# Query and key norms read their sum of squares from an SBUF copy, sample values are transposed three slots later, and the chunk pool has ten buffers

## The chip, the cores and the metric

The kernel runs on one core of one Trainium2 chip. The metric is the time of one execution in device microseconds (us); lower is better. Three runs of the kernel before gave 2138.12, 2135.49 and 2138.64 us, so the median is 2138.12 us.

## What is computed

One step of a decoder layer, for a prompt of 1024 tokens and for 8 samples of 4 tokens each. All 1056 tokens share the weights. The part that matters here is the norm of queries and keys and what attention does with them:

```python
xn = rms_norm(x, norm1_g) * (1 + scale1) + shift1
h, b_gate, c_gate, q, k, v, g_conv, g_att = jnp.split(jnp.dot(xn, w_in), split_at, axis=-1)
...
shp = (nb, ns, N_GROUPS, HEADS_PER_GROUP, HEAD_DIM)      # 3 groups, 8 heads, 64
q = rms_norm(q.reshape(shp), q_norm_g)
k = rms_norm(k.reshape(shp), k_norm_g)
...
if decode: o, lse, kb, vb = dilated_attn_decode(...)     # samples: cache plus new keys and values
else:      o, lse = dilated_attn_prompt(...)             # prompt: blocks of 128, window 128
...
x = x + gate1 * jnp.dot(sigmoid(g_conv) * conv_out + sigmoid(g_att) * attn_out, w_o)
x = x + gate2 * jnp.dot(relu(jnp.dot(xn2, w_mlp_in)) ** 2, w_mlp_out)
```

## The kernel before

Tokens lie along the free dimension in three column chunks of 352, features along the 128 partitions. Each fp32 product is split into a high and a low part, so one output tile of 128 features by 352 tokens takes 24 matmuls of 352 columns (`gemm`, L377: high by high, low by high, high by low, for eight blocks of 128). The stages run one behind the other: modulation and first gates, the convolution inputs, **queries, keys and values with attention beside them** (from about 515 to 1148 us of the profile), the convolution's output product (to about 1283 us), attention's output product, `w_o`, and the two halves of the MLP.

The stage in question goes over 12 units (three attention groups, four pairs of heads each), and in a unit over a query, a key and a value tile with three chunks each. Work beside the matmuls is put into *slots*: `slot()` is called in the middle and at the end of every `gemm`. It runs the functions in `self.later` whose count has run down, then a piece of the attention generator (`bg`), then the paced generators (`decode` for the samples, `merge` for the prompt). Each engine runs what it is given in that order.

A query or key chunk (`qk_epilogue`) has four steps. Right behind its matmuls ScalarE (ACT) writes the squares (`sq`, L688) and copies the raw values (L689) out of the PSUM bank `ps_g`. One slot later VectorE (DVE) splits the squares into a high and a low part (`halves`: `sqh` L160, `sql` L162). Three slots later (`stats`) TensorE (PE) sums the squares over each head with two matmuls (L380, L381) into the PSUM bank `ps_ss`, of which there is **one**, and ACT computes Ln (L389, reads `ps_ss`), Exp (L390) and Square (L391). Another slot later (`scale`) DVE refines the reciprocal root: L395 reads `ps_ss` again, L396 and L706 follow. The bank is free for the next chunk's L380 when L395 has read it.

When a unit's values are done, `begin` calls `sample_values` (a transposition of 32 columns through the PSUM bank `ps_pt`, copied to `vnew` by ACT or DVE as `evac` picks) and then queues the unit's attention. In a group's fourth unit `sample_values` also queues `decode(g)`. `ps_pt`, also a single bank, serves the transpositions of attention (`values`, `att_tr`) too. `chunk()` hands out tiles of 352 columns from a pool with 8 buffers; the epilogues, the decode steps and the gate loads `sg` of the output product live in it. All loads and stores beside a few at the start are issued by SyncE (SP) in program order.

Of the kernel before, what the change touches and what calls it, by code (L numbers as in the profile page):

```python
# [11 lines left out]
AF = mybir.ActivationFunctionType  # L12
ALU = mybir.AluOpType
# [18 lines left out]
EPS = 1e-6  # L32
# [17 lines left out]
class Trunk:  # L50
    def __init__(self, ctx, tc, t):
        self.tc, self.nc, self.t = tc, tc.nc, t
        pool = lambda **kw: ctx.enter_context(tc.tile_pool(**kw))
        self.cp = pool(name="const", bufs=1)
        self.pg = pool(name="pages", bufs=NPG)
        self.ck = pool(name="chunks", bufs=8)
        self.wp = pool(name="weights", bufs=3)
        self.sm = pool(name="small", bufs=3)
        self.pp = pool(name="psum", bufs=1, space=PSUM)
        self.dp = pool(name="scratch", bufs=1, space=DRAM)  # L60
        self.bg = deque()
        self.paced = [deque(), deque()]
        self.pause = [0, 0]
        self.credit = 0.0
        self.rate = 0.0
        self.items = deque()
        self.ready = set()
        self.bias = None
        self.done = False
        self.work = 0.0  # L70
        self.later = []
        self.act_load = 0.0
        self.dve_load = 0.0
# [607 lines left out]
    def qk_epilogue(self, is_k, g, j, c, ps, st):  # L681
        nc = self.nc
        if c == 0:
            st["n"] = self.page("kn" if is_k else "qn")
        qn = st["n"]
        qc = qn[:, c * CH:(c + 1) * CH]
        sq = self.chunk("sq")
        nc.scalar.activation(sq, ps[:, :CH], AF.Square)  # L688
        nc.scalar.copy(qc, ps[:, :CH])  # L689
        h = []  # L690

        def halves():
            h.extend(self.chunk(n, dt=F32R) for n in ("sqh", "sql"))
            self.split(h[0], h[1], sq, CH, hi_on="dve")

        def stats():
            ss = self.bank("ss")[:, :CH]
            self.sumsq_mm(ss, self.blk_r, h[0], h[1], True, True)
            h.clear()
            r0 = self.chunk("r0")  # L700
            self.rstd_a(ss, sq, r0, self.eps[:, 1:2])
            self.later.append((1, lambda: scale(ss, r0)))

        def scale(ss, r0):
            self.rstd_b(r0, ss, sq, r0, 64 * EPS)
            nc.vector.scalar_tensor_tensor(  # L706
                out=qc, in0=qc, scalar=self.qkg[:, is_k:is_k + 1], in1=r0, op0=ALU.mult, op1=ALU.mult)
            if c == 2:
                self.later.append((1, finish))

        def finish():
            hi, lo = self.page("hi", (P, NP), F32R), self.page("lo", (P, NP), F32R)
            st["hi"], st["lo"] = hi, lo
            if g == 0:
                self.split(hi, lo, qn[:, 0:NP], NP, lo_on="pool")
            else:
                d = DIL[g]
                h3, l3 = (a.rearrange("p (r a) -> p r a", r=d) for a in (hi, lo))
                self.split(h3, l3, qn[:, 0:NP].rearrange("p (a r) -> p r a", r=d), NP, lo_on="pool")
            nc.vector.tensor_copy(self.samp[is_k][:, 4 * g + j, :], qn[:, NP:T])  # L720
            if is_k:
                w = (P, 512, NP)[g]
                self.later.append((3, lambda: nc.sync.dma_start(out=self.t["k_out"][g][j], in_=qn[:, NP - w:T])))

        self.later.append((1, halves))
        self.later.append((3, stats))

    def store_v(self, g, j, page):
# [558 lines left out]
    def run(self):  # L1287
        nc, t, c = self.nc, self.t, self.cp
# [47 lines left out]
        st = {}  # L1336
# [18 lines left out]
        st = {}  # L1355
        yc = {}

        def begin(g, j, st):
            self.sample_values(g, j, st["v"]["v"])
            self.add_unit(g, j, st["q"], st["k"], st["v"]["v"])  # L1360
            if (g, j) == units[-1]:
                self.done = True
                self.rate = 2000.0
            else:
                self.rate = self.work / 18 * 0.85

        for ji in range(ji, nb):
            kd, g, j = jobs[ji]
            for ch in range(NCH):
                s = slice(ch * CH, (ch + 1) * CH)  # L1370
                ps = self.bank("g")
                self.gemm(ps[:, :CH], self.wt[ji], range(KD), [(self.xh[k][:, s], self.xl[k][:, s]) for k in range(KD)])
                if ch == 0:
                    st[kd] = {}
                if kd in "qk":
                    self.qk_epilogue(int(kd == "k"), g, j, ch, ps, st[kd])
                else:
                    self.v_epilogue(g, j, ch, ps, st["v"])
                del ps
                if ch == 0:  # L1380
                    self.prep_to(ji + 1, True)
                    if kd == "k":
                        self.bias = self.load_bias(g, j)
                if kd == "v" and ch == 2:
                    self.later.append((2, lambda g=g, j=j, st=st: begin(g, j, st)))
                    st = {}
                if ch == 2:
                    self.wt.pop(ji)
                if (kd, g, j) == ("k", ORDER[2], 3) and ch == 2:
                    yc[0] = self.conv_ops(0)  # L1390
                self.slot()
# [249 lines left out]
        def scale(m, a, t):  # L1641
            k = 2 * H - 32 * t
            nc.scalar.activation(a[:, :k], a[:, :k], AF.Copy, scale=gate2[:, m, 0:1])
            if t:
                s = a[:, k:].rearrange("p (b t) -> p b t", t=NT)
                nc.vector.tensor_tensor(out=s, in0=s, in1=gate2[:, m, 1:9].unsqueeze(2).to_broadcast([P, NB, NT]), op=ALU.mult)
# [60 lines left out]
        g = 0  # L1707
# [35 lines left out]
        for n, (m, ch) in enumerate([(m, ch) for m in (4, 5, 6, 7, 0, 1, 2, 3) for ch in range(NCH)]):  # L1743
            j, s = m % 2, slice(ch * CH, (ch + 1) * CH)
# [230 lines left out]
```

## Time and profile before

| | |
|---|---|
| median of three runs | 2138.12 us |
| profiled execution | 2140.99 us, span 2139.2 us |
| PE busy | 2026.4 us (95%) |
| DVE, ACT, POOL busy | 1422.8, 998.2, 777.5 us (67%, 47%, 36%) |
| mean granted TensorE clock | 0.983 of full speed |

The profile is of one execution; its own time is 2.87 us above the median of the three runs. A busy share is a mean over stages. What a wait costs is read in its stage: from the list of who waited for whom on PE, and from the timeline around the wait. In a timeline row the square brackets at the end give the idle time of the engine just before the instruction, and what ended it.

### The profile page before, as it was taken

What the parts mean: (1) busy time and instruction counts of PE and PEld (TensorE: products, weight loads), DVE (VectorE), ACT (ScalarE), POOL (GpSimd) and SP (SyncE); (2) the same over time, 40 slices, a digit from 0 to 9 for tenths busy, and PEclk for the clock granted to TensorE, in tenths of its full rate; (3) what the DMA queues carried; (4) which work ended last, traced back from release to release, by engine and by line L of the source; (5) the groups of instructions that cost most, each with busy time, mean ns of one, the idle gap of its engine ahead of it and who ended that gap; (6) DMA issues with size and microseconds to landing.
All of it is one profiled execution on the core that took longest, in us unless ns stands there. A gap on an engine that the chain in (4) does not pass through costs nothing. (4 is left out here: it accounts for less than half of the span.)

```text
span 2139.2 us, 38867 instructions
## 1 busy us (share of the span) xinstructions
PE 2026.4 (95%) x15092; PEld 1903.0 (89%) x15092; DVE 1422.8 (67%) x2944; ACT 998.2 (47%) x2193; POOL 777.5 (36%) x544
## 2 busy tenths in 40 slices
PE   5899999999999999999999989999999999999998
PEld 2799999889989888888888889989999998999998
DVE  4847766444666655566676677678444447999997
ACT  4623332434656655555555233455555557433332
POOL 3645655331111111100011114234323335887785
PEclk8899999999999999999999999999999999999999
DMA  7242312664112343433247875642356639555542
GB/s 287 65 144 81 101 62 79 239 218 155 56 56 64 121 127 130 129 124 127 83 144 247 274 254 176 211 148 98 122 200 242 252 115 347 205 207 200 180 166 97
DMA packets 143376, 338.69 MB, mean 158 GB/s; under 512 B 34392, under 2 KB 81112, under 8 KB 142168
## 3 DMA queue, kind: packets, MB, share of 16 engines
q1 hardware_dynamic: 142760, 336.01, 46.5%
q8 instruction: 118, 1.93, 0.4%
q14 instruction: 66, 0.54, 0.1%
q10 hardware_dynamic: 432, 0.20, 0.0%
HBM read 279.00 MB, written 116.39 MB: 185 GB/s over the span
## 5 line engine op out<-in xcount | busy, mean ns | idle before, releaser
L162 DVE TENSOR_TENSOR wprod<-wraw,wprod 128x512 fp32r<-128x512 f32 x276 | 275.0, 997 | 171.5 <-ACT wprod L158 169.9
L377 PE MATMUL ps_g<-xh,whi 128*128 128x352 f32 x1056 | 357.4, 338 | 8.0 <-DVE graw L99 3.8
L377 PE MATMUL ps_g<-xh,wlo 128*128 128x352 f32 x1056 | 346.5, 328 | 7.1 <-DVE wlo L200 7.1
L377 PE MATMUL ps_g<-xl,whi 128*128 128x352 f32 x1056 | 346.3, 328 | 2.4 <-POOL xl L406 1.7
L377 PEld LDWEIGHTS ps_g<-xh,whi 128*128 128x128 f32 x1056 | 203.0, 192 | 32.9 <-issue 13.2
L158 ACT CAST wprod<-wraw 128x512 fp32r<-128x512 f32 x276 | 163.3, 618 | 134.4 <-DVE wprod L162 104.5
L377 PEld LDWEIGHTS ps_g<-xh,wlo 128*128 128x128 f32 x1056 | 202.6, 192 | 8.5 <-DVE wlo L200 8.5
L377 PEld LDWEIGHTS ps_g<-xl,whi 128*128 128x128 f32 x1056 | 203.7, 193 | 4.9 <-POOL xl L406 3.4
L200 DVE TENSOR_TENSOR wlo<-wraw,whi 128x512 fp32r<-128x512 f32 x200 | 152.5, 803 | 50.0 <-ACT whi L193 49.6
L162 POOL TENSOR_TENSOR lo<-qn,hi 128x1024 fp32r<-128x1024 f32 x12 | 32.9, 2739 | 361.7 <-ACT hi L158 326.1
L277 POOL TENSOR_TENSOR ps_z<-ps_z,ps_s 128x264 f32<-128x264 f32 x64 | 63.9, 1001 | 254.4 <-DVE ps_s L276 254.3
L264 PE MATMUL ps_s<-th,wprod 128*128 128x264 f32 x512 | 146.5, 286 | 1.7 <-DVE ps_s L276 1.7
L264 PE MATMUL ps_g<-th,wprod 128*128 128x264 f32 x512 | 146.9, 287 | 0.0
L266 PE MATMUL ps_g<-th,wprod 128*128 128x264 f32 x512 | 146.0, 285 | 0.0
L265 PE MATMUL ps_s<-tl,wprod 128*128 128x264 f32 x512 | 145.9, 285 | 0.0
L265 PE MATMUL ps_g<-tl,wprod 128*128 128x264 f32 x512 | 145.8, 285 | 0.0
L266 PE MATMUL ps_s<-th,wprod 128*128 128x264 f32 x512 | 145.5, 284 | 0.0
L994 ACT ACTIVATE S<-S,ng 128x128 f32<-128x128 f32 (+1 forms) x192 | 84.2, 440 | 111.2 <-DVE ng L989 111.2
L193 ACT CAST whi<-wraw 128x512 fp32r<-128x512 f32 x200 | 113.3, 618 | 41.3 <-DMA wraw<-in_w_conv_out 27.3
L264 PE MATMUL ps_g<-xh,wprod 128*128 128x264 f32 x384 | 110.0, 287 | 2.9 <-ACT wprod L158 2.9
L264 PE MATMUL ps_s<-xh,wprod 128*128 128x264 f32 x384 | 109.3, 285 | 3.4 <-DVE ps_s L280 3.4
L266 PE MATMUL ps_g<-xh,wprod 128*128 128x264 f32 x384 | 109.8, 286 | 0.2 <-DVE wprod L162 0.2
(382 smaller groups left out, 6424.9 us busy)
## 6 DMA issues: line engine op xcount, KB each, us to landing
wraw<-in_w_in SPq DMA_DIRECT2D x76, 512.0 KB, 4.3
wada<-in_w_ada SPq DMA_DIRECT2D x48, 512.0 KB, 5.4
hid_d<-hid SPq DMA_DIRECT2D x32, 528.0 KB, 4.0
wraw<-in_w_mlp_in SPq DMA_DIRECT2D x32, 512.0 KB, 5.6
wraw<-in_w_mlp_out SPq DMA_DIRECT2D x32, 512.0 KB, 3.8
hraw<-hid_d SPq DMA_DIRECT2D x56, 264.0 KB, 4.5
kv<-in_v SPq DMA_DIRECT2D x28, 512.0 KB, 5.9
wraw<-in_w_conv_out SPq DMA_DIRECT2D x24, 512.0 KB, 7.0
```

Source lines behind the costliest of these rows:

```text
L158: nc.scalar.copy(hi, src)
L162: eng.tensor_tensor(out=lo, in0=src, in1=hi.bitcast(F32), op=ALU.subtract)
L193: self.nc.scalar.copy(hi[:, s], w[:, s])
L200: self.nc.vector.tensor_tensor(out=lo[:, s], in0=w[:, s], in1=hi[:, s].bitcast(F32), op=ALU.subtract)
L264: nc.tensor.matmul(ps, hi, xh, start=(k == 0), stop=False)
L265: nc.tensor.matmul(ps, hi, xl, start=False, stop=False)
L266: nc.tensor.matmul(ps, lo, xh, start=False, stop=(k == 3))
L277: nc.gpsimd.tensor_tensor(out=z[p], in0=z[p], in1=s[p], op=ALU.add)
L377: self.nc.tensor.matmul(ps, a, x, start=(i == 0), stop=(i == n - 1))
L994: nc.scalar.activation(s, s, AF.Exp, bias=ng[:, hh, i:i + 1], accum_out=sm[:, hh, i:i + 1])
```

## The change

Three edits. `ScalarE` copies `ps_ss` plus the small constant into `sq` first (L701, Identity), and the rest of the norm, on ACT and on DVE, reads that copy; the intermediate values get a chunk tile `tmp` of their own. `sample_values` is put off by three slots. The chunk pool has ten buffers. No reciprocal root, no matmul and no transfer is added or dropped.

```diff
-        self.ck = pool(name="chunks", bufs=8)
+        self.ck = pool(name="chunks", bufs=10)
...
             h.clear()
-            r0 = self.chunk("r0")
-            self.rstd_a(ss, sq, r0, self.eps[:, 1:2])
-            self.later.append((1, lambda: scale(ss, r0)))
-
-        def scale(ss, r0):
-            self.rstd_b(r0, ss, sq, r0, 64 * EPS)
+            r0, tmp = self.chunk("r0"), self.chunk("tmp")
+            nc.scalar.activation(sq, ss, AF.Identity, bias=self.eps[:, 1:2])
+            nc.scalar.activation(tmp, sq, AF.Ln)
+            nc.scalar.activation(r0, tmp, AF.Exp, scale=-0.5)
+            nc.scalar.activation(tmp, r0, AF.Square, scale=float(0.5 ** 0.5))
+            self.later.append((1, lambda: scale(r0, tmp)))
+
+        def scale(r0, tmp):
+            nc.vector.tensor_tensor(out=tmp, in0=sq, in1=tmp, op=ALU.mult)
+            nc.vector.scalar_tensor_tensor(out=r0, in0=tmp, scalar=1.5, in1=r0, op0=ALU.subtract, op1=ALU.mult)
             nc.vector.scalar_tensor_tensor(
                 out=qc, in0=qc, scalar=self.qkg[:, is_k:is_k + 1], in1=r0, op0=ALU.mult, op1=ALU.mult)
...
         def begin(g, j, st):
-            self.sample_values(g, j, st["v"]["v"])
+            self.later.append((3, lambda: self.sample_values(g, j, st["v"]["v"])))
             self.add_unit(g, j, st["q"], st["k"], st["v"]["v"])
```

How the instructions stand on the engines is shown at three places. The first is ACT at the first two query chunks behind the fourth unit, whose sample values are among those that ACT evacuates (`whi` is a weight's high part, `r` the tile `r0`). Before:

```order
L96 COPY vnew<-ps_pt 32x128
L688 ACTIVATE sq<-ps_g 128x352
L689 COPY qn<-ps_g 128x352
L193 CAST whi<-wraw 128x512 x2
L688 ACTIVATE sq<-ps_g 128x352
L689 COPY qn<-ps_g 128x352
L389 ACTIVATE sq<-ps_ss,eps 128x352
L390 ACTIVATE r_8394<-sq 128x352
L391 ACTIVATE sq<-r_8394 128x352
```

and now:

```order
L688 ACTIVATE sq<-ps_g 128x352
L689 COPY qn<-ps_g 128x352
L193 CAST whi<-wraw 128x512 x2
L688 ACTIVATE sq<-ps_g 128x352
L689 COPY qn<-ps_g 128x352
L96 COPY vnew<-ps_pt 32x128
L701 ACTIVATE sq<-ps_ss,eps 128x352
L702 ACTIVATE tmp<-sq 128x352
L703 ACTIVATE r_8444<-tmp 128x352
L704 ACTIVATE tmp<-r_8444 128x352
```

The copy of the sample values has moved behind the squares and raw copies of two chunks, and four ACT instructions stand where three stood.

The second place is PE in the fifth unit, where the statistics of a query chunk are followed by the transposed values of the unit before (`values`, four transpositions in `ps_pt` and four in `ps_g`). Before:

```order
L377 MATMUL ps_g<-xh,wlo 128x352
L380 MATMUL ps_ss<-sqh,blk_r 128x352
L381 MATMUL ps_ss<-sql,blk_r 128x352
L102 MATMUL ps_pt<-ident,v 128x128 x4
L102 MATMUL ps_g<-ident,v 128x128 x4
L377 MATMUL ps_g<-xh,whi 128x352
```

and now:

```order
L377 MATMUL ps_g<-xh,wlo 128x352
L102 MATMUL ps_pt<-ident,v 32x128
L380 MATMUL ps_ss<-sqh,blk_r 128x352
L381 MATMUL ps_ss<-sql,blk_r 128x352
L102 MATMUL ps_pt<-ident,v 128x128 x4
L102 MATMUL ps_g<-ident,v 128x128 x4
L377 MATMUL ps_g<-xh,whi 128x352
```

The sample transposition, which stood 38 rows further up, now stands two matmuls ahead of the next use of `ps_pt`.

The third place is DVE in the first query tile, from the halves of one chunk to the scaling of the chunk ahead of it. Before:

```order
L160 CAST sqh<-sq 128x352
L162 TENSOR_TENSOR sql<-sq,sqh 128x352
L395 SCALAR_TENSOR_TENSOR sq<-ps_ss,sq 128x352
L396 SCALAR_TENSOR_TENSOR r_5688<-sq,r_5688 128x352
L706 SCALAR_TENSOR_TENSOR qn<-qn,qkg,r_5688 128x352
```

and now:

```order
L160 CAST sqh<-sq 128x352
L162 TENSOR_TENSOR sql<-sq,sqh 128x352
L708 TENSOR_TENSOR tmp<-sq,tmp 128x352
L709 SCALAR_TENSOR_TENSOR r_5688<-tmp,r_5688 128x352
L710 SCALAR_TENSOR_TENSOR qn<-qn,qkg,r_5688 128x352
```

The count and the places of the DVE instructions are the same; the first of the three scaling steps no longer reads `ps_ss`.

## Rows read from the trace of the kernel before

**Rows 1.** Busy time by stretch: PE, PEld, DVE, ACT, POOL, then clock, DMA share, GB/s.
```profile
515.00:1148.00 633.00, 612.85 (x4508) 550.81 (x4506) 400.33 (x1087) 365.06 (x916) 73.44 (x34) 0.99 0.34 107
1148.00:1283.00 135.00, 122.75 (x896) 110.41 (x896) 91.36 (x227) 46.31 (x117) 15.23 (x8) 0.92 0.88 276
```

**Rows 2.** Who PE waited for, 515 to 1300 us: total us, times, longest.
```profile
PE ps_ss L380 <- DVE sq L395: 17.9, 14, 3.2
PE ps_s L1154 <- DMA kv<-in_k1T: 4.2, 2, 3.6
...
PE ps_pt L102 <- ACT vnew L96: 2.7, 1, 2.7
```

**Rows 3.** Timeline of all engines at one wait for the bank: start, us, instruction.
```profile
571.96 0.55 ACT L389 ACTIVATE sq<-ps_ss,eps 128x352 f32<-128x352 f32 x1
...
573.60 0.53 DVE L395 SCALAR_TENSOR_TENSOR sq<-ps_ss,sq 128x352 f32<-128x352 f32 x1 [0.94 <-ACT sq L391]
...
574.18 0.43 PE L380 MATMUL ps_ss<-sqh,blk_r 128*128 128x352 f32 x1 [1.42 <-DVE sq L395]
```

**Rows 4.** The same at another wait, with the statistics of the chunk before.
```profile
956.39 0.32 PE L380 MATMUL ps_ss<-sqh,blk_r 128*128 128x352 f32 x1
...
960.89 0.55 ACT L389 ACTIVATE sq<-ps_ss,eps 128x352 f32<-128x352 f32 x1
961.07 0.53 DVE L162 TENSOR_TENSOR sql<-sq,sqh 128x352 fp32r<-128x352 f32 x1
...
963.11 0.43 PE L380 MATMUL ps_ss<-sqh,blk_r 128*128 128x352 f32 x1 [2.39 <-DVE sq L395]
...
963.77 0.56 ACT L389 ACTIVATE sq<-ps_ss,eps 128x352 f32<-128x352 f32 x1
```

**Rows 5.** Groups by form: line, engine, instruction, count, busy us, mean ns, idle.
```profile
L389 ACT ACTIVATE sq<-ps_ss,eps 128x352 f32<-128x352 f32 x72 | 40.4, 561 | 7.8 <-PE ps_ss L381 7.8
L162 DVE TENSOR_TENSOR sql<-sq,sqh 128x352 fp32r<-128x352 f32 x72 | 37.8, 526 | 3.4
L395 DVE SCALAR_TENSOR_TENSOR sq<-ps_ss,sq 128x352 f32<-128x352 f32 x72 | 37.6, 522 | 29.0 <-ACT sq L391 28.7
L390 ACT ACTIVATE r<-sq 128x352 f32<-128x352 f32 x72 | 35.9, 499 | 2.3
```

**Rows 6.** Busy time behind four waits of PE, columns as in Rows 1.
```profile
634.70:638.70 4.00, 4.00 (x16) 3.78 (x16) 3.35 (x3) 3.46 (x6) 2.56 (x1) 0.57 0.16 62
847.20:853.20 6.00, 6.00 (x20) 6.00 (x21) 3.30 (x14) 3.40 (x13) 0.00 (x0) 0.50 0.57 181
1111.90:1115.90 4.00, 4.00 (x18) 3.62 (x20) 3.86 (x5) 2.49 (x4) 1.98 (x1) 0.60 0.00 0
1151.00:1157.00 6.00, 6.00 (x26) 5.62 (x28) 1.06 (x3) 1.62 (x3) 0.00 (x0) 0.50 1.03 294
```

**Rows 7.** Timeline at the last unit's sample values.
```profile
1150.66 0.25 ACT L96 COPY vnew<-ps_pt 32x128 f32<-32x128 f32 x1
...
1150.96 0.47 PE L102 MATMUL ps_pt<-ident,v 128*128 128x128 f32 x1 [2.66 <-ACT vnew L96]
...
1156.49 0.53 DVE L1419 TENSOR_TENSOR mc<-ps_g,sg 128x352 f32<-128x352 f32 x1 [4.93 <-DMA sg<-gate_d]
```

**Rows 8.** What the copies to `vnew` waited for: us, times.
```profile
  PE ps_pt L102: 15.5, 11
```

**Rows 9.** Timeline, first and last softmax and score transposition of the stage.
```profile
563.44 0.19 ACT L994 ACTIVATION_READ_ACCUMULATOR S<-S,ng 128x1 f32 x1
...
564.76 0.38 PE L102 MATMUL ps_pt<-ident,S 128*128 128x128 f32 x2
...
1135.56 0.19 ACT L994 ACTIVATION_READ_ACCUMULATOR S<-S,ng 128x1 f32 x1
...
1142.15 0.66 PE L102 MATMUL ps_pt<-ident,S 128*128 128x128 f32 x4
```

## Prediction

> **What bounds the kernel now.** I read the busy time by stretch first. In the stage of queries, keys and values (515 to 1148 us) PE is busy 612.85 of 633 us, at a granted clock of 0.99, while DVE has 400 us of work and ACT 365 [rows 1]. PE sets the pace there; the 20 us in which it is not busy, and the time in which it runs at the lower clock, are what an edit outside the matmuls can win. The list of what PE waited for says where these 20 us are: 17.9 us in 14 waits of the first statistics matmul (L380) for DVE's L395, at most 3.2 us each [rows 2]. The other waits of this stage are small. The timeline shows what such a wait is: ACT has read the bank `ps_ss` by 572.51, but the bank is held until L395 has read it too, and L395 starts at 573.60, because it stands behind ACT's Exp and Square and DVE's own queue; PE stood still for 1.42 us [rows 3]. So the chain is statistics, three ACT steps, DVE, next statistics, over a single bank.
>
> In the next stretch (1148 to 1283 us) the limits are others: DMA is at 0.88 and PE loses 12 us and some of its clock [rows 1].
>
> **The release of the bank.** With the change L380 needs two things: ACT's copy of the chunk before (L701, which stands where L389 stands now) and this chunk's `sql` from DVE. Both have times in the trace. I put the end of the previous L389 and of `sql` beside the moment at which PE was ready, for all 71 successive pairs. In 64 pairs both lie over 1 us ahead. Three are late: in rows 4 PE was ready at 960.72 (963.11 less 2.39), `sql` ended at 961.60 and L389 at 961.44, so 0.88 us of the 2.39 remain [rows 4]; the two others keep 0.75 and 0.29 us. In all 1.9 us remain if ACT is no later than now. ACT will be later: see the next part. With every `sql` and copy half a microsecond later the same pairs leave 4.0 us. I take the middle, 2.9 us. So 17.9 − 2.9 = **15.0 us won**.
>
> **The clock behind the waits.** Behind three of the 14 waits PE runs at the lower of its two levels for a while: 4 us at 0.57, 6 us at 0.50 and 4 us at 0.60 [rows 6]. Against full speed that is 4·0.43 + 6·0.50 + 4·0.40 = 6.3 us. Not all of it comes back, since one of the three waits stays in part, and some instructions there don't scale with the clock: I take **5.0 us won**, between 2 and 6.3.
>
> **What ACT and DVE pay.** Per chunk ACT gets one instruction more. The copy reads the bank and adds a constant, as L389 does: 561 ns; Ln now reads SBUF, as Exp does: 499 ns [rows 5]. 72·(561 + 499 − 561) = 35.9 us more on ACT, 365 to 401 of 633 us. The cover is PE's own matmuls: ACT and DVE act between them with room. How much room is read at attention, where PE needs their softmax. The first transposition of the stage starts 1.13 us behind the last softmax row (564.76 against 563.63), the last one 6.40 us behind [rows 9]; of the 44 in the stage all but the first have 3.4 us or more. Half a microsecond per chunk is hidden there, and PE coming earlier by up to 3.2 us at a removed wait nearly always too. Where it isn't, PE waits for what is late next, the softmax or the split of the squares: I set **1.5 us lost**, between 0 and 4.
> DVE's first scaling step changes from one PSUM and one SBUF input (522 ns) to two from SBUF, as in L162 (526 ns) [rows 5]: 72·4 ns = 0.3 us, hidden, and no longer in PE's chain. [...]
>
> **Sample values three slots later.** What moves is the transposition, its evacuation, and in three units `decode(g)`, whose loads (SP's queue), memsets of `dq` (POOL's queue), score and value matmuls and softmax all go three slots down. None is added. *Removed:* the one long wait of PE for a copy to `vnew`, 2.66 us in the last unit, where ACT came to it at 1150.66 behind a softmax and a weight cast [rows 7], and the lower clock behind it, 6·0.50 = 3.0 us [rows 6]: 5.7 us. But what is late next is already in the trace: DVE's product with the gates waits for the load `sg` until 1156.49 [rows 7], which holds a `ps_g` bank, and DMA is at 1.03 there [rows 6]. I count on **2.0 us won**, between 0 and 5.7.
> *Added:* so far these copies waited for PE, not PE for them, in 11 of 12 units [rows 8], because at the old place ACT and DVE had nothing else due. At the new place the copy stands behind the squares and raw copy of the chunk that just ended. In five units (third, fifth, ninth, tenth and twelfth) the next use of `ps_pt` comes within about 1 us of PE work. The copy takes the place that L389 has now, and L389 starts 0.66 us behind its first matmul when ACT is free (963.77 against 963.11) and 4.50 us behind when it isn't (960.89 against 956.39) [rows 4]. With the free case in mind I take 0.9 us where ACT copies and values follow at once (fifth and ninth unit) and 0.5 us in the three others: **3.3 us lost**; the bounds are 0 and 5·4.5 = 22.5 us.
> *Decode later:* in the output stretch PE waited 4.2 us for the keys of the samples [rows 2], with DMA at 0.88 [rows 1]. These loads go behind one or two weight loads. The wait may vanish or double; I take 0, with 4.2 us either way. The last sample transposition now comes in the 23rd of 24 products of that stretch, still inside it, so nothing is left over for its end.
>
> **Ten chunk buffers.** A chunk of query or key takes five tiles in place of four, so ten buffers reach as far as eight did. PE's waits name no chunk tile as what was missing [rows 2]. I take 0.
>
> **The sum.** −15.0 − 5.0 + 1.5 − 2.0 + 3.3 = **−17.2 us**. The profiled execution of 2140.99 us (span 2139.2) would become 2123.8. It lies 2.87 us above the median of the three runs; from the median, 2138.12 − 17.2 = **2120.9 us**, 0.8% less.
>
> **Rivals.**
> *The wait moves to ACT.* The bank is freed by ACT, and ACT has more to do. If ACT falls behind as at 960.89 more often, the copy and, through the squares, `sql` come late, and about half of the 17.9 us and of the clock stay: gain 17.2 − 0.5·(15.0 + 5.0) ≈ 7, 2131 us. For it: 4.50 us of lag at one place, and three pairs late already. Against it: 64 of 71 pairs have over 1 us, and ACT is idle 268 of 633 us.
> *The output stretch takes it back.* PE comes 17 us earlier to a stretch in which DMA is at 0.88. If its loads don't start earlier too, the gain is gone: 2138 us. For it: DMA share over 1 around 1151. Against it: before 1148 DMA is at 0.34 [rows 1], and SP issues in program order as tiles come free, so the loads should move with PE.
> *Slower: PE waits for `vnew`.* The place is the five units named above, the mechanism the single bank `ps_pt` with its copy behind other ACT and DVE work. Without this term the gain is 20.5 us, so it turns into a loss when the five waits cost over 4.1 us each, their lower clock included. At 4.5 us of lag and 1.7 us of clock (5.0 over three waits) they cost 31 us: 2138.1 + 31 − 20.5 = 2149 us; half-way between, 2144. For it: the lag at 960.89, and two of the five copies stand behind a weight cast or attention's work. Against it: the free case is the common one.
>
> **How the numbers follow.** The forecast (bank waits gone, gain 10 to 28) has 0.62, the wait that moves to ACT 0.17, the output stretch 0.11, the slower case 0.10. The best that the bounds allow is 17.9 − 1.9 + 6.3 + 5.7 + 4.2 = 32 us won. The range 2110 to 2136 holds the forecast and the ACT rival, and leaves out about 2 in 10: most of the third and all of the fourth case, and a gain beyond 28. About 0.2% (4.3 us) is what a measurement of this kernel can tell from no change. Faster by more: 0.61 + 0.15 + 0.01 = 0.77; within: 0.13; slower by more: 0.10.
>
> **What would show it.** Right: the list of PE's waits has L380 with under 5 us in all, now for DVE's `sql` or ACT's L701, and the granted clock near 637, 850 and 1113 is 1.0. ACT has some 36 us more in this stage, and the stage is about 18 us shorter, with the same length from its end to the end of the kernel. The sample copies show as PE waits of L102 for `vnew` in up to five units, about 1 us each. Wrong: L380 still waits over 8 us; or the stretch after the stage is longer by what the stage won; or L102's waits for `vnew` add up to over 10 us.

## The result and the profile after

The change made the kernel slower: 2158.6 us (four runs, 2152.6 to 2163.4) against 2138.4 us beside it, a ratio of 1.0086, 95% interval 1.0068 to 1.0104. A second group of runs gave 2157.3 us and 1.0076 (1.0060 to 1.0092). The forecast was 2120.9 us, faster, with a range up to 2136. The profiled execution of after, 2152.64 us with a span of 2150.9, is the fastest of its runs; it is 11.7 us above the profiled one of before, and the ledger below is made for these two. The medians lie 20 us apart, so some 9 us of the loss don't show between these two executions; a second profile of after (2157.68 us, in the table under Experiments) has the same stage and 3.7 us more in the output stretch.

The stage of queries, keys and values, from its first to its last projection matmul, took 625.9 us before and takes 639.5 us. What lies ahead of it is 2.7 us shorter, what lies behind it 0.8 us longer. So the loss is inside the stage that was to become 18 us shorter. Of its 13.6 us, 10.2 are time in which PE waits (30.24 against 20.05 us) and 5.1 are lost to the clock: the time for which the granted clock was low, weighted by how much was missing, adds up to 12.0 against 6.8 us. What is left of the stage is no longer than before, 597.3 against 599.0 us. By busy time (stretch; PE, PEld, DVE, ACT, POOL; clock, DMA share, GB/s), to be laid beside [rows 1]:

```profile
515.00:1148.00 633.00, 602.02 (x4406) 540.42 (x4405) 395.90 (x1060) 391.94 (x978) 71.48 (x33) 0.98 0.33 106
1148.00:1283.00 135.00, 122.75 (x934) 110.14 (x932) 87.13 (x229) 45.77 (x114) 15.21 (x8) 0.95 0.85 268
```

PE is 11 us less busy in the same 633 us, and its clock a hundredth lower. Who PE waited for between 515 and 1148 us (total us, times, longest), beside [rows 2]:

```profile
PE ps_s L1194 <- DVE st L990: 9.6, 5, 3.3
PE ps_s L1158 <- DVE st L990: 4.2, 3, 1.9
PE ps_ss L380 <- ACT sq L701: 3.7, 3, 2.2
PE ps_s L1145 <- DVE st L990: 3.0, 2, 2.1
PE ps_s L1191 <- DVE st L990: 2.8, 1, 2.8
PE ps_ss L380 <- ACT whi L193: 2.4, 1, 2.4
...
PE ps_pt L102 <- ACT vnew L96: 1.3, 2, 0.7
```

The waits for the statistics bank did shrink, from 17.9 to 6.1 us. But the four lines with L990 are new: matmuls of `decode` (L1145, L1158, L1191, L1194) wait for a bank `ps_s` until DVE's L990 has read it, 19.6 us in 11 waits. In before such waits (there L1154 for L986) were one line of 1.8 us:

```profile
PE ps_s L1154 <- DVE st L986: 1.8, 2, 0.9
```

One of the new places in the timeline of all engines of after (start, us, instruction, idle before it):

```profile
843.74 0.28 PE L984 MATMUL ps_s<-lo,hi 64*128 64x128 f32 x2
843.85 0.28 PE L984 MATMUL ps_s<-hi,lo 64*128 64x128 f32 x2
843.92 0.58 DVE L710 SCALAR_TENSOR_TENSOR kn<-kn,qkg,r 128x352 f32<-128x352 f32 x1
844.43 1.01 DVE L99 COPY O<-ps_o 128x512 f32<-128x512 f32 x1
...
845.29 0.27 DVE L990 CUSTOM_DVE_ANT_0 S<-ps_s,bias 128x128 f32<-128x128 f32 x1
...
846.04 1.07 PE L1194 MATMUL ps_s<-kv,dq 128*32 128x512 f32 x8 [1.92 <-DVE st L990]
...
847.04 0.43 PE L377 MATMUL ps_g<-xh,whi 128*128 128x352 f32 x1
```

Attention's scores (L984) fill both `ps_s` banks. A step of `decode` stands directly behind them in PE's order and needs one back. DVE first finishes the norm's scaling and the copy of an attention output, then reads the scores; PE stands for 1.92 us, and the projection behind it (L377) too. Three slots later moved `decode` to these places: of its 34 groups of matmuls on `ps_s`, 10 stand in the same slot as scores in after, 2 in before. Nine of the 11 waits are at these places; the two others (0.9 and 1.6 us) have half a projection product between the scores and `decode`.

### The profile page after: what moved, and what is told of

Its sections match the earlier page's. It is cut to its first block, busy times and chain, and to the rows that moved or that the text cites. A ratio compares the mean times of both kernels' runs of the same rounds, so it can differ in the third digit from the quotient of the medians.

```text
span 2150.9 us, 38951 instructions
## 1 busy us (share of the span) xinstructions
PE 2026.2 (94%) x15092; PEld 1903.2 (88%) x15092; DVE 1421.4 (66%) x2943; ACT 1030.9 (48%) x2266; POOL 777.5 (36%) x544
## 4 chain that ended last, share of the span: by engine, by line
PE 51%; DVE 20%; ACT 6%; issue 3%; DMA 2%; POOL 1%; SPq 0%; DVEq 0%; ACTq 0%; POOLq 0%
PE ps_g L377 24%; DVE acc L1742 4%; DVE wprod L162 4%; PE ps_g L264 3%; PE ps_g L266 3%; PE ps_s L265 3%; PE ps_g L265 3%; PE ps_s L266 3%; PE ps_s L264 3%; DVE wlo L200 2%; DVE hl L1594 1%; PE ps_s L984 1%; PE ps_o L1026 1%; PE ps_pt L102 1%; DVE S L990 1%
## 5 line engine op out<-in xcount | busy, mean ns | idle before, releaser
L162 DVE TENSOR_TENSOR wprod<-wraw,wprod 128x512 fp32r<-128x512 f32 x276 | 273.8, 993 | 169.4 <-ACT wprod L158 169.2
L377 PE MATMUL ps_g<-xh,whi 128*128 128x352 f32 x1056 | 355.7, 337 | 8.0 <-DVE graw L99 3.8
L377 PE MATMUL ps_g<-xh,wlo 128*128 128x352 f32 x1056 | 345.9, 328 | 7.4 <-DVE wlo L200 7.4
L377 PE MATMUL ps_g<-xl,whi 128*128 128x352 f32 x1056 | 345.9, 328 | 1.4 <-POOL xl L406 0.7
L377 PEld LDWEIGHTS ps_g<-xh,whi 128*128 128x128 f32 x1056 | 202.9, 192 | 33.2 <-issue 18.6
L377 PEld LDWEIGHTS ps_g<-xh,wlo 128*128 128x128 f32 x1056 | 202.6, 192 | 8.6 <-DVE wlo L200 8.6
L377 PEld LDWEIGHTS ps_g<-xl,whi 128*128 128x128 f32 x1056 | 203.7, 193 | 3.6 <-POOL xl L406 2.1
L162 POOL TENSOR_TENSOR lo<-qn,hi 128x1024 fp32r<-128x1024 f32 x12 | 33.2, 2767 | 357.2 <-ACT hi L158 296.6
L264 PE MATMUL ps_s<-th,wprod 128*128 128x264 f32 x512 | 145.8, 285 | 1.7 <-DVE ps_s L276 1.7
L265 PE MATMUL ps_g<-tl,wprod 128*128 128x264 f32 x512 | 145.8, 285 | 0.0
L998 ACT ACTIVATE S<-S,ng 128x128 f32<-128x128 f32 (+1 forms) x192 | 84.2, 441 | 107.2 <-DVE ng L993 107.2
```

The lines of the kernel that those rows point to most:

```text
L162: eng.tensor_tensor(out=lo, in0=src, in1=hi.bitcast(F32), op=ALU.subtract)
L264: nc.tensor.matmul(ps, hi, xh, start=(k == 0), stop=False)
L265: nc.tensor.matmul(ps, hi, xl, start=False, stop=False)
L377: self.nc.tensor.matmul(ps, a, x, start=(i == 0), stop=(i == n - 1))
L998: nc.scalar.activation(s, s, AF.Exp, bias=ng[:, hh, i:i + 1], accum_out=sm[:, hh, i:i + 1])
```

## Experiments

Ratios are to runs of the kernel before in the same group, with 95% intervals. The groups ran on different chips, so runs of different groups are compared by their ratios. "PE waits" and "stage" are of the profiled execution, from the first to the last projection matmul of the stage; "output" goes from there to the last product of the output stretch. All in us.

| run | time | ratio | PE waits | stage | output |
|---|---|---|---|---|---|
| before | 2138.4 to 2142.0 | 1 | 20.1 | 625.9 | 144.2 |
| after | 2158.6 | 1.0086 (1.0068–1.0104) | 30.2 | 639.5 | 144.9 |
| after again | 2157.3 | 1.0076 (1.0060–1.0092) | 30.2 | 639.4 | 148.6 |
| norm edit only | 2141.2 | 1.0000 (0.9990–1.0010) | 20.3 | 629.6 | 142.7 |
| norm edit, 8 buffers | 2138.8 | 1.0004 (0.9994–1.0014) | 20.2 | 628.2 | 143.1 |
| sample values only | 2149.6 | 1.0045 (1.0029–1.0062) | 26.2 | 631.1 | 145.8 |
| decode later only | 2153.6 | 1.0056 (1.0043–1.0069) | 28.8 | 630.7 | 148.1 |
| after, decode at its old slot | 2146.0 | 1.0024 (1.0014–1.0035) | 20.9 | 625.9 | 146.1 |
| after, decode kept off scores | 2152.5 | 1.0051 (1.0038–1.0064) | 23.0 | 629.3 | 150.4 |
| the same, last decode old | 2149.0 | 1.0052 (1.0039–1.0065) | 23.1 | 629.4 | 151.4 |
| norm edit, zeroing on VectorE | 2139.3 | 0.9991 (0.9981–1.0000) | 18.9 | 622.9 | 140.9 |
| norm edit, exponentials later | 2120.0 | 0.9899 (0.9885–0.9914) | 8.7 | 610.3 | 137.6 |
| before, exponentials later | 2119.0 | 0.9910 (0.9897–0.9924) | 10.0 | 609.7 | 138.1 |
| after, exponentials later | 2149.6 | 1.0048 (1.0035–1.0060) | 26.8 | 635.0 | 142.4 |
| the same, decode kept off | 2126.2 | 0.9952 (0.9940–0.9964) | 11.9 | 612.5 | 141.9 |
| the same, decode at old slot | 2124.0 | 0.9941 (0.9929–0.9953) | 10.8 | 610.9 | 143.2 |
| norm, exponentials, zeroing | 2112.9 | 0.9879 (0.9866–0.9893) | 6.0 | 603.9 | 140.6 |
| that, decode kept off scores | 2109.0 | 0.9867 (0.9854–0.9880) | 3.6 | 602.0 | 137.2 |

In all 18 profiles the stage less PE's waits and less what the clock lost is 594.5 to 599.5 us, so what the runs change there are these two.

The theories that are told apart: **A**, decode's matmuls behind attention's scores wait for `ps_s`; **B**, ScalarE's added instruction delays what PE wants; **C**, the late transposition of the sample values costs it. After the first group **D** came up, that the bank was only the last link of a chain, with **E** (as B: ScalarE's added work eats the gain) and **F** (the two edits pay only together) against it, and **G**, that the output stretch is where the loss lies.

**The parts of the change.** After again:

> The changed kernel once more, beside the others of this group. If the 2158.6 us of its first runs is the kernel's own time, 2152 to 2163 us again, with a mean granted clock of 0.978 to 0.983, under that of before; if it was the chip, 2142 to 2150 us.

2157.3 us: the loss is the kernel's own, and the mean clock of these runs is 0.9815 against 0.9859 of before. The norm edit alone is after with one line put back:

```diff
-            self.later.append((3, lambda: self.sample_values(g, j, st["v"]["v"])))
+            self.sample_values(g, j, st["v"]["v"])
```

> The norm edit and the ten chunk buffers alone; sample_values stays where it was before. Theory A (the loss is the decode steps: queued three slots later, their matmuls stand directly behind attention's scores and wait for the two ps_s banks until VectorE has read the scores): the decode steps stand as before, so the gain of the norm edit is left alone. In the trace of after the ps_ss waits fell from 17.9 to 6.1 us, so 11 to 16 us below before: 2122 to 2128 us, and PE's ps_s waits on L990 stay near 2 us. Rival B (the loss is the fifth ScalarE instruction, which comes late for the norms and weights that PE wants): about as slow as after, 2150 to 2160 us. Rival C (the loss is the late transposition of the sample values): as theory A.

Theory A's 2122 to 2128 us are missed: the edit wins nothing, 2141.2 us. Nor did it lose what B says. PE's first waits in the stage:

```profile
PE ps_ss L380 <- ACT sq L701: 11.8, 5, 5.3
PE ps_ss L380 <- ACT whi L193: 2.3, 1, 2.3
PE ps_s L1158 <- DVE st L990: 1.8, 2, 0.9
```

Fourteen waits have become six, but with 14.1 us in all, and the longest is 5.3 where it was 3.2. With eight buffers in the pool, the same:

```diff
-        self.ck = pool(name="chunks", bufs=10)
+        self.ck = pool(name="chunks", bufs=8)
```

> The norm edit alone with the chunk pool left at eight buffers. If the ten buffers neither win nor cost anything: as the norm edit with ten, ratio to before 0.998 to 1.002. If the edit needs them (its second chunk page per norm would then wait for a free one): slower than that by 4 us or more.

So the pool is worth nothing either way. The other half, before with sample_values three slots later:

> Before with nothing changed but sample_values three slots later. Theory A: the ps_s waits on attention's reduction rise from 2 to about 20 us and nothing is won on ps_ss, so above before by 18 to 30 us: 2156 to 2168 us, slower than after. Rival B: as before, 2138 us within 4. Rival C: as theory A, but with the added waits on the transposition's bank ps_pt and not on ps_s.

9.7 us slower. Theory A's place is right (14.4 us on `ps_s` for L986), its size is not: the waits for the bank `ps_ss` fell from 17.9 to 8.4 us at the same time, without any edit to the norm. The two largest lines of its list:

```profile
PE ps_ss L380 <- DVE sq L395: 8.4, 6, 3.1
PE ps_s L1190 <- DVE st L986: 7.6, 5, 3.0
```

Where PE is held at `decode`, the norm catches up. Waits of the two kinds stand in for each other, so they can't be summed as separate prices.

**Which half of the move.** `decode` queued from `begin` at the old place, with the rest of the change, and before with only `decode` queued later:

```diff
             self.later.append((3, lambda: self.sample_values(g, j, st["v"]["v"])))
+            self.queue_decode(g, j)
```

```diff
             self.sample_values(g, j, st["v"]["v"])
+            self.later.append((3, lambda: self.queue_decode(g, j)))
```

> The whole change, but the decode of a group is queued at its old place; only the transposition of the sample values is three slots later. Theory A: as the norm edit alone, 2120 to 2128 us, with the ps_s waits near 2 us. Rival B and rival C: as after, 2150 to 2160 us.

> Before with one thing changed: the decode of a group is queued three slots later; the transposition of the sample values stays at its old place. Theory A (most of the loss is decode's place behind attention's scores): 2146 to 2154 us, like the whole move of sample_values alone (2149.6). Rival C (the late transposition itself costs it): 2139 to 2143 us, as before.

Decode alone costs 0.56%, about 12 us, as much as the whole move. In its profile, 10.2 us longer than that of before, 4.8 us of this lie in the stage and 3.8 in the output stretch. The late transposition costs less: the whole change without late decode is 0.24% (5 us) above before, short of theory A's 2120 to 2128 because the norm edit gives nothing. This run and after differ in nothing but the place of `decode`: its stage is 625.9 us long, 13.5 us shorter than that of after and the same as before's, so in after the whole loss of the stage goes with that place.

**Keeping decode off the scores.** A flag set by `att_scores` lets a decode step wait for the next slot; a second run also puts the last group's `decode` at its old place.

```diff
-            while lane and self.pause[i] <= 0:
+            while lane and self.pause[i] <= 0 and (i or not self.scored):
```

> The whole change, with one rule added: a decode step is put off by a slot where attention's scores were issued in the same slot. In the order no decode step stands directly behind scores then (10 in after, 2 in before). Theory A: the ps_s waits on L990 fall under 3 us, and the time to 2120 to 2130 us. Rivals B and C: as after, 2150 to 2160 us.

> As the run that keeps decode steps out of the slots with scores (2152.5 us), but the last group's decode is queued at its old place; the first two groups stay three slots late. Theory G (what that run still loses lies in the output stretch, where the last group's decode and its transfers come three slots later and the weights behind them too: 150.2 us there against 144.1): the output stretch is back to 142 to 146 us and the time at 2141 to 2147 us, as with the norm edit alone. If the loss lies in the QKV stage, 2149 to 2154 us.

The stage did shrink by 10 us, and the `ps_s` waits on DVE to 6.0 us, not under the 3 that theory A expected. Both times are 0.5% above before, the first in the range of rivals B and C, and the output stretch is the longest of all. Theory G is wrong as well, since the old place of the last decode didn't shorten it. In the first run PE waits there 12.0 us for weights (6.3 for `whi`, 5.7 for `wlo`). Why this stretch is 6 and 7 us longer than before's in these two is open; the two profiles of after differ there by 3.7 us already. So these two runs don't show what keeping `decode` off the scores is worth; further down it is tried again.

**Where the norm edit's gain went.** The 5.3 us wait of the norm edit alone, all engines:

```profile
844.38 2.90 POOL L162 TENSOR_TENSOR lo<-qn,hi 128x1024 fp32r<-128x1024 f32 x1 [24.34 <-ACT hi L158]
...
847.22 0.53 POOL L1129 MEMSET dq<- 128x512 f32 x1
...
847.78 1.45 DVE L1134 COPY dq<-samp 64x16 f32<-64x16 f32 x8 [4.63 <-POOL dq L1129]
...
849.48 0.53 DVE L708 TENSOR_TENSOR tmp<-sq,tmp 128x352 f32<-128x352 f32 x1
...
851.44 0.28 DVE L990 CUSTOM_DVE_ANT_0 S<-ps_s,bias 128x128 f32<-128x128 f32 x1
...
852.60 0.40 ACT L998 ACTIVATE S<-S,ng 128x128 f32<-128x128 f32 x1 [7.11 <-DVE ng L993]
...
854.15 0.44 ACT L688 ACTIVATE sq<-ps_g 128x352 f32<-128x352 f32 x1
854.50 0.43 ACT L689 COPY kn<-ps_g 128x352 f32<-128x352 f32 x1
...
854.83 0.55 ACT L701 ACTIVATE sq<-ps_ss,eps 128x352 f32<-128x352 f32 x1
...
855.43 0.66 PE L380 MATMUL ps_ss<-sqh,blk_r 128*128 128x352 f32 x1 [5.34 <-ACT sq L701]
```

Read from below: PE waits for the bank copy L701; it stands on ACT behind the next chunk's square and copy, these behind attention's exponentials (L998), for which ACT idled 7.11 us; they wait for DVE's maxima (L990, L993); and DVE was held by a zeroing on POOL, behind POOL's 2.9 us split. In before PE was caught at the same chain one chunk earlier, for 3.2 us, and ACT idled as long in front of the exponentials (there L994):

```profile
844.92 1.44 DVE L1130 COPY dq<-samp 64x16 f32<-64x16 f32 x8 [5.33 <-POOL dq L1125]
...
847.19 0.66 PE L380 MATMUL ps_ss<-sqh,blk_r 128*128 128x352 f32 x1 [3.18 <-DVE sq L395]
...
849.73 0.40 ACT L994 ACTIVATE S<-S,ng 128x128 f32<-128x128 f32 x1 [7.12 <-DVE ng L989]
```

With that wait gone PE runs one chunk further and meets the exponentials. Two edits cut the chain at different links, both on top of the norm edit. The first zeroes on VectorE:

```diff
-            nc.gpsimd.memset(qp[:, 0:512], 0.0)
+            nc.vector.memset(qp[:, 0:512], 0.0)
```

> The norm edit alone (2141.2 us), with decode's zeroing of the query page done by VectorE, not GpSimd, where it stood behind a 2.9 us split and held VectorE for 4.6 us at 843. Theory D (the bank ps_ss was only the last link of a chain: VectorE's burst in an attention slot, then the exponentials on ScalarE, then the next square, copy and bank copy behind them; with the last link gone PE runs on and stands at the next step of the same chain): the longest ss wait, 5.3 us, falls under 3 and the slow clock behind it goes, so 2133 to 2138 us. Rival E (ScalarE's 36 us more of work eats the gain everywhere): no change, 2139 to 2143 us.

The second issues the exponentials one slot later, or just ahead of the transposition of their scores if that comes first:

```diff
-                nc.scalar.activation(s, s, AF.Exp, bias=ng[:, hh, i:i + 1], accum_out=sm[:, hh, i:i + 1])
+        def exps():
...
+                    nc.scalar.activation(s, s, AF.Exp, bias=ng[:, hh, i:i + 1], accum_out=sm[:, hh, i:i + 1])
...
+        self.later.append((1, exps))
```

> The norm edit alone, with attention's exponentials issued one slot later, so that the next square, its copy and the copy that frees ps_ss stand ahead of them on ScalarE. Theory D: the ss waits fall from 14.1 to under 6 us, with the slow clock behind them, so 2126 to 2135 us; the transpositions of the scores may wait for the later exponentials, up to 3 us of that. Rival E (ScalarE's added work): ScalarE does the same work, so 2139 to 2143 us.

The zeroing is worth little, 2139.3 us, and the wait at this place is still 4.0 us: outside D's range, at the edge of E's. The exponentials are worth 21 us. That is 6 us more than D's range allowed and far outside E's, with all of ScalarE's added work in place; so E is wrong, and D has the place but not the size. In the stage the waits for L701 are gone; the one left for the bank is (lines are one further down here)

```profile
PE ps_ss L381 <- DVE sqh L161: 2.9, 1, 2.9
```

Then the same without the norm edit:

> Before, with attention's exponentials issued one slot later and nothing else: the norms keep the first copy's old form, in which VectorE's multiply frees ps_ss. Theory D (the chain through the exponentials held PE, and the bank was its last link): the exponentials no longer stand ahead of the first ScalarE step of the norm, so most of the 22 us come without the norm edit too: 2120 to 2128 us. Rival F (the two edits are worth something only together, since either of the two queues alone holds the bank): 2134 to 2142 us.

2119.0 us, 1 us under D's range and far from F's. The ratio is 0.9910 against 0.9899 with the norm edit: the intervals overlap, so the norm edit adds nothing that can be told from noise even here. Without it PE still waits 7.8 us for the bank, in eight waits:

```profile
PE ps_ss L381 <- DVE sq L396: 7.8, 8, 3.2
```

With the edit one wait of 2.9 us is left, and the stage is no shorter (610.3 against 609.7 us).

**Decode again, with the chain out of the way.**

> The whole change with the exponentials one slot later. Theory D with A (decode's place behind the scores costs what it costs, and the exponentials have no part in it): the ss waits go, the ps_s waits on VectorE's reduction stay at 15 to 20 us, so 2120 plus the 11 to 16 us that the late sample values cost: 2131 to 2140 us. If the exponentials were behind decode's waits as well: 2120 to 2126 us.

> The whole change with the exponentials one slot later and with decode steps kept out of the slots with scores. Beside the same without that rule (2149.6 us; its PE waits in the QKV stage are nearly all decode's, 21.3 of 26.8 us, with 13.7 us of clock lost). Theory A: 2120 to 2130 us. Rival C (the late transposition of the sample values, or where decode lies in the output stretch): 2140 to 2150 us.

> The whole change with the exponentials one slot later, and decode queued at its old place, so that of the move of sample_values only the late transposition is left. Theory A: 2119 to 2126 us. Rival C: 2140 us or more.

With the exponentials moved the whole change is at 2149.6 us, not 2131 to 2140: the late sample values now cost 1.5%, some 32 us; a reading that fits is that no other wait takes a share any more. The first of PE's waits of that kernel (L1204 is L1194 of after), and then of the same with decode kept off the scores (lines two further down):

```profile
PE ps_s L1204 <- DVE st L991: 10.7, 5, 3.3
PE ps_s L1168 <- DVE st L991: 5.3, 3, 3.0
PE ps_s L1201 <- DVE st L991: 2.8, 1, 2.8
PE ps_s L1155 <- DVE st L991: 2.4, 2, 2.1
```

```profile
PE ps_pt L1101 <- DVE dS L1098: 3.2, 1, 3.2
PE ps_s L1206 <- DVE st L993: 2.4, 3, 1.6
```

21.2 us of `ps_s` waits fall to 3.1 us (2.4 and two below a half, which are not shown), and the time by 1.0%, some 21 us. The clock of the stage shows the rest, first without the rule and then with it:

```profile
515.00:1148.00 633.00, 605.72 (x4434) 545.11 (x4434) 396.03 (x1067) 394.71 (x983) 71.58 (x33) 0.98 0.34 107
```

```profile
515.00:1148.00 633.00, 618.76 (x4602) 556.83 (x4601) 406.56 (x1109) 406.49 (x1011) 74.42 (x34) 0.99 0.37 116
```

Here only that rule is added, and theory A holds with place and size. Decode at its old slot gives nearly the same, 2124.0 us, 1.1% or some 23 us below. What this last run keeps above the 2120.0 us of the norm edit with late exponentials is the late transposition, 0.4% by the ratios.

**The best version.** The norm edit with the exponentials later, the zeroing on VectorE and sample values at their old place; then with decode kept off the scores:

> The norm edit, the exponentials one slot later and the zeroing on VectorE. The two were worth 1.8 and 21 us apart; theory D has both on one chain, so together a little less than the sum: 2116 to 2121 us, with the QKV stage's PE waits at 8 us or less.

> The best kernel so far (norm edit, exponentials one slot later, zeroing on VectorE: 2112.9 us, ratio 0.988) with decode steps kept out of the slots with scores, 2 of 34 there. Theory A: the 1.8 us of ps_s waits go: 2109 to 2113 us. If the moved steps only meet another wait, 2113 to 2117 us.

2112.9 and 2109.0 us, 1.2% and 1.3% below before. The first is 3 us under its expected range. By the ratios the zeroing, worth 2 us at best alone, is worth some 4 us behind the moved exponentials, and keeping `decode` off the scores some 3 us more; the intervals of neighbours overlap, so neither step alone is clear of noise. In the last kernel PE waits 3.6 us in the stage, and its clock there is 1.00:

```profile
515.00:1148.00 633.00, 628.92 (x4724) 565.77 (x4722) 419.69 (x1148) 413.06 (x1035) 74.86 (x31) 1.00 0.39 122
```

## Why the prediction was wrong

**Decode later, taken as 0 with 4.2 either way.** This is the first step that failed, and the one that turned the sign. It looked at the loads of `decode` alone and priced them in the output stretch. The matmuls of `decode` were named among what moves, but their new neighbours on PE were not looked at. Measured: 12 us alone, 11 to 13 us inside the whole change, 21 to 23 us where the exponentials no longer hold PE. That a wait for `ps_s` on L986 cost 1.8 us before, in two places, was in the trace; how many places there would be, in the order. None of the three signs of being wrong showed in after: they watched L380 (6.1 us, between the bounds of 5 and 8), the output stretch (0.6 us longer) and `vnew` (1.3 us), not `decode`. The slower outcome that had a chance of 0.10 was another mechanism.

**The release of the bank, 15.0 us won.** Of the 17.9 us, 6.1 are left in after, but 14.1 with the norm edit alone, and the time is unchanged. This is the second step that failed. The pairs were compared with PE arriving when it did in before, and the copy and `sql` at most half a microsecond later; a PE that keeps the time of each removed wait arrives earlier at everything behind it. What is late next was the square and the copy behind attention's exponentials, on ACT. The rival in which the wait moves to ACT is what happened, all of it where the rival had half. That after shows only 6.1 us is no success of the edit: sample values moved alone took 9.5 us out of the same list.

**The clock, 5.0 us won.** Nothing came back: in the profiled executions the clock is 0.98 in the stage in after and with the norm edit alone, 0.99 before, and both lose 12.0 us to it where before lost 6.8. It is 1.00 with the exponentials moved in before, and in the best version. But it doesn't follow the sum of the waits: `decode` later alone has 28.8 us of them and loses 3.4 us to the clock.

**What ACT and DVE pay.** Right in size. The forms are as forecast (mean ns of one before the last bar):

```profile
L701 ACT ACTIVATE sq<-ps_ss,eps 128x352 f32<-128x352 f32 x72 | 40.5, 562 | 5.7 <-PE ps_ss L381 5.6
...
L702 ACT ACTIVATE tmp<-sq 128x352 f32<-128x352 f32 x71 | 35.4, 498 | 2.3
```

Forecast were 561 and 499 [rows 5]. DVE's first scaling step (L708) takes 0.52 or 0.53 us in 67 of 71 cases in this window, as L395 did [rows 5]; two take 2.6 us beside a POOL step, which L395 never did (see the last section). ACT's extra work is no cause of the loss: the norm edit alone is at 1.0000, and the work is still there in the fastest kernel.

**Sample values, 2.0 won and 3.3 lost.** The slower rival, PE waiting for `vnew` at five places, didn't come: 1.3 us in two waits. The 2.66 us of [rows 7] are gone. What was named as late next, the product with the gates waiting for its load, did come, with another victim:

```profile
1165.84 0.52 DVE L1423 TENSOR_TENSOR mc<-ps_g,sg 128x352 f32<-128x352 f32 x1 [5.18 <-DMA sg<-gate_d]
1166.29 0.68 DVE L99 COPY vt<-ps_pt 128x512 f32<-128x512 f32 x1
```

The copy of the values stands behind it on DVE, and PE's transposition of the scores at 1167.02 waited 4.03 us for that copy. In sum the late transposition costs 5 us, and 9 with the exponentials moved; 1.3 were forecast.

**Ten chunk buffers, 0.** Right: 1.0000 with ten and 1.0004 with eight.

**The sum.** The norm edit was to win 18.5 us (15.0 and 5.0, less 1.5) and wins 0. Sample values were to lose 1.3 and lose 5, `decode` was at 0 and loses 11 to 13. These are differences from kernel to kernel on the way from before to after, so they add up to the loss by themselves, 16 to 18 us by the two ratios of after; the 12 us of `decode` alone, measured on before, is a value of its own and agrees.

## What to carry to other kernels

A wait that is removed hands PE its time, and PE carries it to the next thing that is late (here a wait of 3.2 us became one of 5.3 us a chunk later): follow the chain behind the wait (here POOL's zeroing, DVE's maxima, ACT's exponentials, then the norm) and try it link by link. What paid here was to take the norm's short steps on ACT out from behind the exponentials (21 us); the last link, the release of the bank, was worth nothing, and the zeroing near the chain's head 2 us at best. Whatever is put off by some slots has new neighbours: list, on the engine that sets the pace, who stands directly behind whom on a shared bank, before and after. Waits on one pace-setting engine can stand in for each other, so that one edit's price depends on whether another wait is still there (decode's place cost 11 to 13 us with the exponentials in the way, 21 to 23 without).

## What the runs showed of the hardware

In after, some DVE instructions that start while POOL is in a two-input step of 2.4 to 3.2 us (the split of queries or keys, L162, or L1277) last until POOL is done: sixteen of them end 0.02 to 0.50 us behind POOL's step. One of them:

```profile
636.47 2.91 POOL L162 TENSOR_TENSOR lo<-qn,hi 128x1024 fp32r<-128x1024 f32 x1 [35.33 <-ACT hi L158]
...
636.74 2.86 DVE L160 CAST sqh<-sq 128x352 fp32r<-128x352 f32 x1 [0.61 <-ACT sq L688]
...
639.70 0.53 DVE L162 TENSOR_TENSOR sql<-sq,sqh 128x352 fp32r<-128x352 f32 x1
```

The cast takes 0.33 to 0.35 us in 69 of its 72 cases; here it ends 0.22 us behind POOL's split. Fourteen of the sixteen are stretched like this by 1.7 to 2.6 us, two by 1.2. L990, which reads PSUM, is not: it takes 0.27 or 0.28 us beside the split at 844.76, and 0.28 at 859.40 with no split running. What holds the stretched ones, no run shows. In after one more step is stretched: L708 has both inputs in SBUF, and two of its 72 took 2.6 us beside L1277. L395, with one input in PSUM, took 0.51 to 0.53 us in all its 72, but none of these started inside such a step earlier than 0.06 us from its end, so they don't show what L395 would take there. In before L396, the next step, took 2.42 and 2.44 us beside the same POOL step (there L1273). The stretching as such was there before the change too (the cast takes 2.76 us at 540.21 of before), and whether moving these steps off POOL would win anything was not tried.
